# A hybrid attention and RWKV-7 layer: how the planner emits side work, where pair set-up waits, and where the gates stand

## The chip, the cores and the metric

The kernel runs on one core of one Trainium2 chip. The metric is the device time of one execution in microseconds; each kernel is run several times and the median is taken. One further execution is profiled, and its trace gives the rows below. In the rows PE is TensorE (PEld its weight loads), DVE is VectorE, ACT is ScalarE, POOL is GpSimd, and SPq is the DMA queue that SyncE (SP) issues to. TensorE's clock has two levels, 1.2 and 2.4 GHz; the rows show the granted level as 0.50 or 1.00.

## The reference

One decoder layer over 512 tokens of width 2048, in float32. An RMS norm of `x`, then one input projection (2048 x 8480) whose columns are attention q, k, v and gate z, the RWKV-7 columns r, k, v with three low-rank parts, and the RWKV gate z. Attention has 16 heads of 64 with rotary q and k, and mixes three dilated causal windows. RWKV-7 has 16 heads whose 64 x 64 state follows

```
sa    = state @ a_t
state = state * w_t + outer(sa, b_t) + outer(v_t, k_t)
y_t   = state @ r_t
```

with the decay `w_t` between 0 and 1 from data, `a_t = -kk`, `b_t = kk * a`, `kk` normalised per head. The result is normalised per head, a bonus is added, and it is multiplied by its low-rank gate `g`. Each branch is multiplied by `silu(z)`; both are concatenated and go through one output projection (2048 x 2048), the residual is added, and a final RMS norm follows.

## The kernel before

All large products are done in pairs of rounded parts: the activations are held as `hth` + `htl`, each weight chunk is loaded as `raw` and split into `whi` (ScalarE) and `wlo` (VectorE), and three matmuls (`hh,whi`, `hl,whi`, `hh,wlo`) make one product. A projection of 128 columns ("main matmuls" `mm_r`, `mm_k`, `mm_v`, `mm_z`, `mm_qk`) is 16 x 3 = 48 matmuls of 128x512. Chunks are loaded and split ahead by `Feeder.tick` at fixed places of this stream (AHEAD = 2 chunks).

The stream of main matmuls is written out by hand in `items` (lines 1215 to 1275): the low-rank columns and k0, then for pair p = 0 to 7 (two RWKV heads of 64 on 128 partitions) k, r and v, with some z projections of the attention gate between; the rest of z0 to z6; `gl128`; three blocks of v for attention (`mv`); 16 blocks of q and k; z8 to z15 (RWKV gates); z7; and then the output projection `mo`, `mh`, `mt` over 16 mixed tiles.

Everything else is a Python generator in `sides`, and `pump` (line 353) runs these between main matmuls while the program is written. `Model` keeps a planned clock: TensorE's calls move it, each other engine has a planned `busy` time from a fixed cost and a cost per element, and a generator's `yield (delay, tile or engine)` sets when it is due again on that clock. Nothing of this runs on the chip: it fixes the order in which each engine's queue is filled. Engines take their queues in order and wait for each other by semaphores. `until(cond)` moves the planned clock in steps of 0.2 us and runs only sides until the condition holds; `drain()` runs sides until none is left; `after(2, f)` runs `f` two matmuls later.

For each pair the sides are:

- `pre(p)`: the normaliser, decays `W` = exp(-cum) and `wi` = exp(cum), the tiles `bt` and `Fa`, the matmuls `pM`, from which `mc` goes to DRAM (`md`) and comes back as the table `Mp`; then the bonus `bn`, and after pair p-1 is `built` the tiles `L`, `X`, `FT` and `A`.
- `subst(p)`, called the solve here: on POOL 31 steps of two products each (`Xtmp`, `XT`) invert the triangles held in `Mp`. Each step needs the one before. It ends in `solved`, and XT goes through DRAM (`xq`).
- `merges(p)`, `build(p)`, `scan(p)`: small matmuls (`zpb`, `zf`, `gp`) that end in `built`, then eight scan steps `Y` one after another, each with two copies on ScalarE or VectorE, which end in `scanned`; then the head's norm, and the tile goes to DRAM as y.

Buffers come from rings: `k2` (20 tiles of 128x512), `k1` (6 small ones), `k4` (9). `shift_evac` takes a projection out of PSUM: a memset of one column of `u` on POOL, a product with `rstd` into `u`, and two operations that make `d`. The z0 to z6 gates go to DRAM (`spill_out`) and come back in `att` (`fetch_y`); z7's is applied after attention. `gate_g(p)` loads the low-rank gate's weights `gw`, splits them (`gh`, `gl`), multiplies (`pg`) and scales the reloaded y; `gate(8+p)` then applies z. `pre_mix` drains, reloads seven attention tiles and starts `mix_split`, which splits the 16 mixed tiles for the output projection in the order `KO` (RWKV first).

Of the kernel before, what the change touches and what calls it, by code (L numbers as in the profile page):

```python
# [11 lines left out]
F32 = mybir.dt.float32  # L12
# [3 lines left out]
ALU = mybir.AluOpType  # L16
# [25 lines left out]
class Model:  # L42


    def __init__(self):
        self.clock, self.ready, self.read = 0.0, {}, {}

# [15 lines left out]
class Engine:  # L63
    def __init__(self, model, eng, fixed, rate):
        self.model, self.eng, self.fixed, self.rate, self.busy = model, eng, fixed, rate, 0.0

    def cost(self, op, o, args):
        rate = self.rate
        if op == "reciprocal":
            rate = 0.0062  # L70
        elif op == "memset":
            return 0.04 + 0.0009 * math.prod(o.shape[1:])
        elif op in ("tensor_scalar", "tensor_copy") and self.fixed == 0.07:
            rate = 0.0006
        return self.fixed + rate * math.prod((args[0] if op == "tensor_reduce" else o).shape[1:])

# [16 lines left out]
class Tensor(Engine):  # L93
# [4 lines left out]
    def __getattr__(self, op):  # L98
        fn = getattr(self.eng, op)

        def call(o, lhs, rhs, **kw):
            m = self.model
            rows = o.shape[0]
            load = rows * 0.00084
            passes = 2 if rhs.dtype != F32R and op == "matmul" else 1
            hold = math.prod(rhs.shape[1:]) * (1 if rhs.dtype == F32R else 2) / 2400
            if rows < P and o.offset >= 64 * 512:
                hold, passes = 0.02, 1
            w = max(m.after([], [lhs, rhs]), m.read.get(o.name, 0.0))
            for _ in range(passes):  # L110
                self.start = max(m.clock, self.start + load, w)
                m.clock = self.start + hold + 0.003
            m.done(m.clock, [o], [lhs, rhs], 0.2)
            return fn(o, lhs, rhs, **kw)  # L114
        return call
# [14 lines left out]
def hymba_kernel(ctx: ExitStack, tc: tile.TileContext, xT, x, wa, wb, wo, pv, w2a2, g2, fg,  # L130
# [3 lines left out]
    model = Model()  # L134
    V = Engine(model, nc.vector, 0.07, 0.00104)
    S = Engine(model, nc.scalar, 0.06, 0.00095)
    G = Engine(model, nc.gpsimd, 0.15, 0.0020)
    TE = Tensor(model, nc.tensor)
# [11 lines left out]

    K1N, K2N, K4N, RAWN, AHEAD = 6, 20, 9, 2, 2

# [41 lines left out]
    def prologue():  # L194
# [7 lines left out]
        def squares():  # L202
            for k in range(KT):
# [5 lines left out]
                if k % 2:  # L209
                    yield 0.0, S  # L210
            yield 0.0, acc
            yield from rms(acc)
# [140 lines left out]
    def pump():  # L353
# [4 lines left out]
        for s_ in sorted(sides, key=lambda s: (s[2], s[1])):  # L358
            while s_[1] <= model.clock and credit[0] > (-DEBT, 0, -99.0)[s_[2]]:
                t = model.clock  # L360
                try:
                    wait = next(s_[0])
# [165 lines left out]
    def shift_evac(src, mu, name, rows=P, scaled=True):  # L528
        u = k2([P, T + 1], f"u_{name}")
        G.memset(u[:rows, 0:1], 0.0)  # L530
        if scaled:
# [77 lines left out]
    def pre(p, r, k, v):  # L609
# [71 lines left out]
        Q.dma_start(md.rearrange("c p t -> p c t"), mc)  # L681
        while p >= 1 and p - 1 not in solved:
            yield 0.5
# [12 lines left out]
        V.scalar_tensor_tensor(rk, r, col("r_k", p), k, ALU.mult, ALU.mult)  # L696
        yield 0.1, rk
        rh, rl = hilo(rk, f"rk{p}")
        yield 0.1, rl
# [11 lines left out]
        for h in range(2):  # L711
            S.copy(X[h][H[h], :, H[h]], ident[H[h], H[h]][:, None, :].to_broadcast([64, NCH, C]))
            V.tensor_tensor(L[h][H[h], :, H[1 - h]], c3(k)[H[h]], wi[H[h]], ALU.mult)
            G.tensor_tensor(X[h][H[h], :, H[1 - h]], c3(r)[H[h]], W[H[h], :, 1:C + 1], ALU.mult)
        yield 0.1, L[0], L[1]
# [26 lines left out]
    def subst(p, Mp, rn2):  # L742
        while p >= 1 and p - 1 not in solved:
            yield 0.287
        V.tensor_tensor(Mp, Mp, rn2[:, None, :].to_broadcast([P, 32, 32]), ALU.mult)
        XT = sp.tile([P, 8, 32], F32, tag="XT", bufs=1, name=f"XT{p}")
        tmp = sp.tile([P, 8, 32], F32, tag="Xtmp", bufs=1, name=f"Xtmp{p}")
        G.memset(XT, 0.0)
        for g in range(4):
            V.tensor_copy(XT.rearrange("p c t -> p (c t)")[32 * g:32 * g + 32, 8 * g:8 * g + 232:33],  # L750
                          rn2[32 * g:32 * g + 32, 8 * g:8 * g + 8])
        yield 0.1, XT
        for j in range(31):
            n = 31 - j
# [366 lines left out]

    KO = list(range(8, 16)) + list(range(8))
    mh, ml = [], []
# [91 lines left out]
    add_aa((0, 9), ("lora", "k0"), (lora_evac, lambda a: rkv_evac(0, "k", 8, a)))  # L1215
    NZ, EARLY = 7, {2: 1, 3: 1, 4: 1, 5: 1, 6: 1}
    zs = iter(range(NZ))
# [7 lines left out]
    for p in range(NP):  # L1225
        add_z(EARLY.get(p, 0))
        add_call(lambda p=p: until(lambda: p < 3 or p - 3 in scanned))
        if p:
# [17 lines left out]
    for p in range(NP):  # L1246
        add_call(lambda p=p: start(gate_g(p), 0.21))
        add_a(50 + p, f"z{8 + p}", lambda a, p=p: gate(8 + p, a))
    for p in range(NZ, NP):
        add_call(lambda p=p: fetch_y(p, f"o{p}"))  # L1250
        if p == NP - 1:
            add_call(lambda: pre_mix())
        add_a(42 + p, f"z{p}", lambda a, p=p: gate(p, a))

    def pre_mix():
# [57 lines left out]
def _layout(inp):  # L1313
# [27 lines left out]
    wo = f["w_out"][0].reshape(KT, P, 4, 512)  # L1341
    wo = wo[list(range(8, 16)) + list(range(8))].transpose(2, 1, 0, 3)
    mu = f["shift_mu"][0]
# [41 lines left out]
```

## Time and profile before

| | |
|---|---|
| median of 3 runs | 1188.93 us (1188.77 to 1189.62) |
| the profiled execution | 1189.53 us, its span 1187.7 us |
| mean granted TensorE clock | 0.982 |
| TensorE busy | 1144.1 us (96%) |
| VectorE busy | 738.8 us (62%) |
| ScalarE busy | 537.2 us (45%) |
| POOL busy | 354.2 us (30%) |

The span runs from the first to the last instruction of the profiled execution, and the rest of its own time lies around it. Busy time of TensorE is the union of its matmuls, whose ends overlap, so a busy TensorE need not be one at its peak. A line number such as L114 or L86 is that of the planner's wrapper through which every matmul or vector operation passes, so rows are told apart by the names of their tiles.

### The profile page before, as it was taken

What the parts mean: (1) busy time and instruction counts of PE and PEld (TensorE: products, weight loads), DVE (VectorE), ACT (ScalarE), POOL (GpSimd) and SP (SyncE); (2) the same over time, 40 slices, a digit from 0 to 9 for tenths busy, and PEclk for the clock granted to TensorE, in tenths of its full rate; (3) what the DMA queues carried; (4) which work ended last, traced back from release to release, by engine and by line L of the source; (5) the groups of instructions that cost most, each with busy time, mean ns of one, the idle gap of its engine ahead of it and who ended that gap; (6) DMA issues with size and microseconds to landing.
All of it is one profiled execution on the core that took longest, in us unless ns stands there. A gap on an engine that the chain in (4) does not pass through costs nothing. (4 is left out here: it accounts for less than half of the span.)

```text
span 1187.7 us, 19122 instructions
## 1 busy us (share of the span) xinstructions
PE 1144.1 (96%) x6878; PEld 948.2 (80%) x6878; DVE 738.8 (62%) x1475; ACT 537.2 (45%) x1196; POOL 354.2 (30%) x629
## 2 busy tenths in 40 slices
PE   7899999999999989979999999999999999999997
PEld 5687877787787778858899888888887878888897
DVE  6678667777886756786745455666667646334252
ACT  6354536555535545554534323445345434223133
POOL 1007566574838082383800021110010000011010
PEclk9899999999999979998999999999999999999999
DMA  7243333424241414314233544444354336344333
GB/s 259 82 117 113 97 108 87 123 71 125 74 137 55 139 46 116 108 59 111 58 96 90 163 125 146 132 127 127 116 154 133 113 107 217 113 140 121 110 125 142
DMA packets 89583, 139.10 MB, mean 117 GB/s; under 512 B 37904, under 2 KB 47632, under 8 KB 89488
## 3 DMA queue, kind: packets, MB, share of 16 engines
q1 hardware_dynamic: 89056, 137.31, 38.3%
q8 instruction: 54, 0.88, 0.3%
q10 hardware_dynamic: 432, 0.58, 0.1%
q14 instruction: 41, 0.34, 0.1%
HBM read 114.18 MB, written 14.48 MB: 108 GB/s over the span
## 5 line engine op out<-in xcount | busy, mean ns | idle before, releaser
L86 POOL TENSOR_TENSOR Xtmp<-XT,Mp 128x248 f32<-128x248 f32 (+30 forms) x248 | 127.9, 516 | 126.9 <-DVE XT L86 109.0
L86 POOL TENSOR_TENSOR XT<-XT,Xtmp 128x248 f32<-128x248 f32 (+30 forms) x248 | 139.8, 564 | 21.1 <-DVE XT L86 2.1
L114 PE MATMUL mm_z<-hl,whi 128*128 128x512 f32 x256 | 103.3, 404 | 0.0
L114 PE MATMUL mm_z<-hh,whi 128*128 128x512 f32 x256 | 102.9, 402 | 0.0
L114 PE MATMUL mm_z<-hh,wlo 128*128 128x512 f32 x256 | 102.4, 400 | 0.0
L114 PE MATMUL mm_qk<-hh,whi 128*128 128x512 f32 x256 | 100.6, 393 | 0.8 <-ACT gtok L86 0.8
L114 PE MATMUL mm_qk<-hh,wlo 128*128 128x512 f32 x256 | 100.8, 394 | 0.0
L114 PE MATMUL mm_qk<-hl,whi 128*128 128x512 f32 x256 | 100.4, 392 | 0.0
L86 DVE TENSOR_TENSOR wlo<-raw_o,whi 128x512 fp32r<-128x512 f32 x64 | 48.1, 793 | 83.4 <-ACT whi L86 83.3
L86 POOL TENSOR_TENSOR y<-y,fg 128x512 f32<-128x512 f32 (+1 forms) x16 | 19.3, 1242 | 264.4 <-ACT mo L86 245.7
L86 ACT ACTIVATE ss<-ss,nm 128x128 f32<-128x128 f32 (+3 forms) x64 | 35.5, 555 | 101.4 <-DVE nm L86 101.4
L86 ACT ACTIVATE whi<-raw_o 128x512 fp32r<-128x512 f32 x64 | 36.8, 623 | 92.6 <-PE mo L114 69.9
L86 POOL TENSOR_TENSOR m<-m,m 128x512 f32<-128x512 f32 x16 | 23.0, 1457 | 185.6 <-DVE m L86 161.4
L114 PE MATMUL mv<-whi,hh 128*128 128x352 f32 x192 | 64.8, 337 | 10.9 <-DVE u_gl L86 9.5
L114 PE MATMUL mo<-whi,mh 128*128 128x512 f32 x192 | 74.7, 389 | 0.0
L114 PE MATMUL mo<-wlo,mh 128*128 128x512 f32 x192 | 74.7, 389 | 0.0
L114 PE MATMUL mo<-whi,ml 128*128 128x512 f32 x192 | 74.7, 389 | 0.0
L86 DVE TENSOR_TENSOR wlo<-raw_qk,whi 128x512 fp32r<-128x512 f32 x64 | 48.5, 783 | 36.5 <-ACT whi L86 34.3
L86 DVE TENSOR_TENSOR wlo<-raw_v,whi 128x352 fp32r<-128x352 f32 (+1 forms) x80 | 49.2, 630 | 34.7 <-ACT whi L86 34.0
L114 PE MATMUL mv<-wlo,hh 128*128 128x352 f32 x192 | 64.0, 333 | 0.0
L86 DVE TENSOR_TENSOR wlo<-raw_z,whi 128x512 fp32r<-128x512 f32 x64 | 47.4, 766 | 26.3 <-ACT whi L86 26.0
L114 PE MATMUL mv<-whi,hl 128*128 128x352 f32 x192 | 63.4, 330 | 0.0
(297 smaller groups left out, 3024.2 us busy)
## 6 DMA issues: line engine op xcount, KB each, us to landing
raw_z<-in_wa_dram SPq DMA_DIRECT2D x32, 512.0 KB
raw_qk<-in_wa_dram SPq DMA_DIRECT2D x32, 512.0 KB
raw_o<-in_wo_dram SPq DMA_DIRECT2D x32, 512.0 KB
raw_v<-in_wb_dram SPq DMA_DIRECT2D x24, 352.0 KB
raw_r<-in_wa_dram SPq DMA_DIRECT2D x16, 512.0 KB
raw_v<-in_wa_dram SPq DMA_DIRECT2D x16, 512.0 KB
raw_k<-in_wa_dram SPq DMA_DIRECT2D x15, 512.0 KB
xk<-in_xT_dram SPq DMA_DIRECT2D x16, 256.0 KB
```

The lines of the kernel that those rows point to most:

```text
L86: return fn(o, *args, **kw)
L114: return fn(o, lhs, rhs, **kw)
```

## The change

The planner's costs are new: each TensorE matmul of the rounded type moves the planned clock by 0.0135 us beyond its columns instead of 0.003, a change of matmul shape by 0.1, VectorE and ScalarE have a least cost (0.18, 0.25), and POOL's cost is 0.30 + 0.0028 per element instead of 0.15 + 0.0020. `pump` starts no step of a side with rank 0 or 1 while VectorE or ScalarE is planned busy for more than 3 us ahead. `Mp` is loaded once pair p-2 is solved instead of p-1, and `subst` scales it and sets up XT (now two buffers) before it waits for solve p-1. In `pre`, r and k are multiplied by `W` and `wi` in place on all 128 partitions, and their halves are copied into `X` and `L`. The memset in `shift_evac` is on VectorE. `k1` has five buffers. All eight attention gates z0 to z7 are projected in the recurrent part, one ahead of each of pairs 2 to 7, and pairs 4 to 7 wait for pair p-3 to be built where pairs 3 to 7 waited for it to be scanned. `pre_mix` stands before z15, and the output projection takes its mixed tiles in the order 0 to 15. The rms step of the start is due 2 us of plan later.

```diff
--- before.py
+++ after.py
@@ -43,7 +43,7 @@
     def __init__(self):
-        self.clock, self.ready, self.read = 0.0, {}, {}
+        self.clock, self.mode, self.ready, self.read = 0.0, None, {}, {}
@@ -61,8 +61,9 @@
 class Engine:
-    def __init__(self, model, eng, fixed, rate):
+    def __init__(self, model, eng, fixed, rate, least=0.0):
         self.model, self.eng, self.fixed, self.rate, self.busy = model, eng, fixed, rate, 0.0
+        self.least = least
@@ -72,7 +73,8 @@
             rate = 0.0006
-        return self.fixed + rate * math.prod((args[0] if op == "tensor_reduce" else o).shape[1:])
+        n = math.prod((args[0] if op == "tensor_reduce" else o).shape[1:])
+        return max(self.least, self.fixed + rate * n)
@@ -107,9 +109,14 @@
             w = max(m.after([], [lhs, rhs]), m.read.get(o.name, 0.0))
+            mode = (lhs.shape[0], rows)
+            if mode != m.mode:
+                m.clock += 0.1
+                m.mode = mode
+            gap = 0.0135 if rhs.dtype == F32R else 0.003
             for _ in range(passes):
                 self.start = max(m.clock, self.start + load, w)
-                m.clock = self.start + hold + 0.003
+                m.clock = self.start + hold + gap
             m.done(m.clock, [o], [lhs, rhs], 0.2)
@@ -132,9 +139,9 @@
     model = Model()
-    V = Engine(model, nc.vector, 0.07, 0.00104)
-    S = Engine(model, nc.scalar, 0.06, 0.00095)
-    G = Engine(model, nc.gpsimd, 0.15, 0.0020)
+    V = Engine(model, nc.vector, 0.07, 0.00106, 0.18)
+    S = Engine(model, nc.scalar, 0.06, 0.00095, 0.25)
+    G = Engine(model, nc.gpsimd, 0.30, 0.0028)
     TE = Tensor(model, nc.tensor)
@@ -148,7 +155,7 @@
-    K1N, K2N, K4N, RAWN, AHEAD = 6, 20, 9, 2, 2
+    K1N, K2N, K4N, RAWN, AHEAD = 5, 20, 9, 2, 2
@@ -208,7 +215,7 @@
                     yield 0.0, S
-            yield 0.0, acc
+            yield 2.0, acc
             yield from rms(acc)
@@ -358,6 +365,8 @@
                 t = model.clock
+                if s_[2] >= 0 and max(V.busy, S.busy) > t + 3.0:
+                    break
                 try:
@@ -527,7 +536,7 @@
         u = k2([P, T + 1], f"u_{name}")
-        G.memset(u[:rows, 0:1], 0.0)
+        V.memset(u[:rows, 0:1], 0.0)
         if scaled:
@@ -679,7 +688,7 @@
         Q.dma_start(md.rearrange("c p t -> p c t"), mc)
-        while p >= 1 and p - 1 not in solved:
+        while p >= 2 and p - 2 not in solved:
             yield 0.5
@@ -695,6 +704,8 @@
         yield 0.1, rk
+        V.tensor_tensor(c3(r), c3(r), W[:, :, 1:C + 1], ALU.mult)
+        V.tensor_tensor(c3(k), c3(k), wi, ALU.mult)
         rh, rl = hilo(rk, f"rk{p}")
@@ -710,8 +721,8 @@
             S.copy(X[h][H[h], :, H[h]], ident[H[h], H[h]][:, None, :].to_broadcast([64, NCH, C]))
-            V.tensor_tensor(L[h][H[h], :, H[1 - h]], c3(k)[H[h]], wi[H[h]], ALU.mult)
-            G.tensor_tensor(X[h][H[h], :, H[1 - h]], c3(r)[H[h]], W[H[h], :, 1:C + 1], ALU.mult)
+            evac(L[h][H[h], :, H[1 - h]], c3(k)[H[h]])
+            evac(X[h][H[h], :, H[1 - h]], c3(r)[H[h]])
         yield 0.1, L[0], L[1]
@@ -740,16 +751,16 @@
     def subst(p, Mp, rn2):
-        while p >= 1 and p - 1 not in solved:
-            yield 0.287
         V.tensor_tensor(Mp, Mp, rn2[:, None, :].to_broadcast([P, 32, 32]), ALU.mult)
-        XT = sp.tile([P, 8, 32], F32, tag="XT", bufs=1, name=f"XT{p}")
+        XT = sp.tile([P, 8, 32], F32, tag="XT", bufs=2, name=f"XT{p}")
         tmp = sp.tile([P, 8, 32], F32, tag="Xtmp", bufs=1, name=f"Xtmp{p}")
...
         yield 0.1, XT
+        while p >= 1 and p - 1 not in solved:
+            yield 0.1
         for j in range(31):
@@ -1119,7 +1130,7 @@
-    KO = list(range(8, 16)) + list(range(8))
+    KO = list(range(16))
     mh, ml = [], []
@@ -1213,7 +1224,7 @@
     add_aa((0, 9), ("lora", "k0"), (lora_evac, lambda a: rkv_evac(0, "k", 8, a)))
-    NZ, EARLY = 7, {2: 1, 3: 1, 4: 1, 5: 1, 6: 1}
+    NZ, EARLY = 8, {2: 1, 3: 1, 4: 1, 5: 1, 6: 1, 7: 1}
     zs = iter(range(NZ))
@@ -1224,7 +1235,7 @@
         add_z(EARLY.get(p, 0))
-        add_call(lambda p=p: until(lambda: p < 3 or p - 3 in scanned))
+        add_call(lambda p=p: until(lambda: p < 4 or p - 3 in built))
         if p:
@@ -1245,13 +1256,9 @@
         add_call(lambda p=p: start(gate_g(p), 0.21))
-        add_a(50 + p, f"z{8 + p}", lambda a, p=p: gate(8 + p, a))
-    for p in range(NZ, NP):
-        add_call(lambda p=p: fetch_y(p, f"o{p}"))
         if p == NP - 1:
             add_call(lambda: pre_mix())
-        add_a(42 + p, f"z{p}", lambda a, p=p: gate(p, a))
-
+        add_a(50 + p, f"z{8 + p}", lambda a, p=p: gate(8 + p, a))
     def pre_mix():
@@ -1339,7 +1346,7 @@
     wo = f["w_out"][0].reshape(KT, P, 4, 512)
-    wo = wo[list(range(8, 16)) + list(range(8))].transpose(2, 1, 0, 3)
+    wo = wo.transpose(2, 1, 0, 3)
     mu = f["shift_mu"][0]
```

## Rows read from the trace of the kernel before

**Rows 1.** The page, part 1: busy us, share of the span, instructions.

```profile
PE 1144.1 (96%) x6878; PEld 948.2 (80%) x6878; DVE 738.8 (62%) x1475; ACT 537.2 (45%) x1196; POOL 354.2 (30%) x629
```

**Rows 2.** Busy time by stretch: length, busy us (instructions) by engine, PEclk, DMA.

```profile
core 0: us, PE busy (x) PEld busy (x) DVE busy (x) ACT busy (x) POOL busy (x), PEclk, DMA share, GB/s
43.20:50.00 6.80, 6.80 (x19) 5.54 (x20) 4.09 (x20) 0.00 (x0) 0.00 (x0) 0.50 0.51 151
...
155.80:159.20 3.40, 3.40 (x10) 2.63 (x9) 2.45 (x8) 0.88 (x2) 2.59 (x4) 0.50 0.20 17
...
330.00:360.00 30.00, 30.00 (x230) 24.13 (x228) 24.57 (x50) 13.26 (x27) 14.75 (x22) 1.00 0.42 115
...
413.65:422.10 8.45, 6.83 (x59) 5.80 (x57) 6.89 (x16) 6.02 (x13) 6.85 (x10) 1.00 0.44 141
422.10:435.62 13.52, 10.83 (x56) 8.93 (x57) 4.55 (x8) 3.97 (x11) 12.38 (x20) 0.50 0.13 39
435.62:439.10 3.48, 3.48 (x37) 2.71 (x37) 2.21 (x4) 1.09 (x2) 3.01 (x7) 0.50 0.00 0
...
531.30:541.50 10.20, 5.12 (x17) 5.13 (x18) 7.51 (x21) 4.88 (x11) 2.32 (x12) 0.50 0.30 72
690.00:960.00 270.00, 269.71 (x1334) 219.20 (x1333) 171.45 (x427) 125.30 (x347) 19.99 (x14) 1.00 0.43 128
```

**Rows 3.** Timeline of TensorE: start, duration, operation, idle time before it and releaser.

```profile
42.69 1.45 PE L114 MATMUL pr<-ones,acc 128*128 128x1 f32 x8 [3.59 <-DVE acc L86]
...
154.15 0.69 PE L114 MATMUL zpb<-xd,zsb 32*32 32x32 f32 x32 [1.93 <-DVE zsb L86]
...
324.16 1.15 PE L114 MATMUL pM<-Fa,bt 64*64 64x64 f32 x32 [1.90 <-DVE wc L86]
...
415.23 4.05 PE L114 MATMUL gp<-X,L 128*128 128x128 f32 x32
...
435.62 0.77 PE L114 MATMUL mm_k<-hh,whi 128*128 128x512 f32 x1
...
536.38 0.66 PE L114 MATMUL mv<-whi,hh 128*128 128x352 f32 x1 [9.45 <-DVE u_gl L86]
```

**Rows 4.** Waits of TensorE: total us, times, longest us.

```profile
PE pF L114 <- DVE L L86: 2.9, 6, 1.1
```

**Rows 5.** Timeline of VectorE around 535 us.

```profile
535.63 0.69 DVE L86 TENSOR_TENSOR u_gl<-mm_gl,rstd 128x512 f32<-128x512 f32 x1
```

**Rows 6.** Timelines of POOL and SP's queue, from solve 4 to solve 5.

```profile
386.82 0.24 POOL L86 TENSOR_TENSOR XT<-XT,Xtmp 128x8 f32<-128x8 f32 x1
...
408.50 1.73 SPq L126 DMA_DIRECT2D Mp<-md  x4
...
414.27 0.61 POOL L86 TENSOR_TENSOR Xtmp<-XT,Mp 128x248 f32<-128x248 f32 x1 [22.68 <-DVE XT L86]
...
454.75 0.22 POOL L86 TENSOR_TENSOR XT<-XT,Xtmp 128x8 f32<-128x8 f32 x1
```

**Rows 7.** Instruction groups, 60 to 660 us: count | busy us, mean ns | idle before.

```profile
L86 POOL TENSOR_TENSOR Xtmp<-XT,Mp 128x248 f32<-128x248 f32 (+30 forms) x248 | 127.9, 516 | 126.9 <-DVE XT L86 109.0
L86 POOL TENSOR_TENSOR X<-d_r,W 64x512 f32<-64x512 f32 x16 | 21.3, 1331 | 0.6
L86 DVE TENSOR_TENSOR L<-d_k,wi 64x512 f32<-64x512 f32 x16 | 17.3, 1080 | 0.3
L86 ACT COPY X<-csts 64x512 f32<-64x512 f32 x16 | 9.8, 613 | 0.1
```

**Rows 8.** Timelines of SP's queue, TensorE and VectorE around z15.

```profile
976.39 2.49 SPq L126 DMA_DIRECT2D gw<-in_g_dram  x5
...
980.45 0.39 PE L114 MATMUL mm_z<-hh,whi 128*128 128x512 f32 x1
...
982.77 0.69 DVE L86 SCALAR_TENSOR_TENSOR yl<-zt,yl 128x512 f32<-128x512 f32 x1
...
987.19 0.60 DVE L86 TENSOR_TENSOR gl<-gw,gh 128x128 fp32r<-128x128 f32 x2
...
991.33 0.39 PE L114 MATMUL pg<-g128h,gh 128*128 128x512 f32 x1
```

## The prediction

> **What bounds the kernel now.** The page's busy table comes first: TensorE is busy 1144.1 of 1187.7 us [rows 1]. At most 43.6 us of idle time is left, and any gain must come from there or from stretches in which the same matmuls run at a lower clock. So the table of windows is read next, for busy time and granted clock by stage [rows 2]. From 690 to 960 us TensorE is busy 269.71 of 270 us at clock 1.00: nothing can be won there, only lost. The losses sit before 660 us, in the recurrent part, and the timeline of TensorE names them one by one [rows 3]. I price each as idle time plus half of what was busy at clock 0.50 (1.2 instead of 2.4 GHz).
>
> - Start, 39 to 50 us: 3.59 idle, waiting for `acc` on VectorE, then 6.80 busy at 0.50, costing 3.40. Together 7.0.
> - 152 to 159: 1.93 idle for `zsb`, then 3.40 at 0.50, costing 1.70. Together 3.6.
> - 324: 1.90 idle for `wc`, without a fall of the clock in the rows that follow.
> - 413.65 to 439.10: no main matmul starts before 435.62, only small ones such as `gp`. Busy are 6.83 at full clock, 10.83 and 3.48 at half, which is 6.83 + 5.42 + 1.74 = 14.0 of work in 25.45. Loss 11.5.
> - 526 to 541: 9.45 idle for `u_gl`, then 5.12 busy at 0.50, costing 2.56. Together 12.0.
> - Short waits of the `pF` matmuls for `L`: 2.9 in six places [rows 4].
>
> The sum is 38.9 us. That is all the change can win in the stages it touches, unless it also removes work, and it removes no matmul.
>
> **Why the two large losses are there.** At 413 the list stands in an `until` (line 1227): pair 7's projections wait until pair 4 is scanned. Only the scan's chain of small matmuls is left to issue, each waiting for a copy on ScalarE or VectorE, and the clock falls. At 526 the last `mv` group needs the PSUM bank that `u_gl` empties. VectorE reaches `u_gl` only at 535.63 [rows 5]. Line 1235 had held the main matmuls until pair 7 was `half` done, which line 682 ties to the end of solve 6, and meanwhile everything that was ready had been put on VectorE ahead of `u_gl`.
>
> Behind both is the solve on POOL. Its last step of pair 4 ends at 387.06 and the first of pair 5 starts at 414.27, of which POOL spent 22.68 waiting for VectorE's `XT`; the table load `Mp` was issued only at 408.50 [rows 6]. Over six such places these waits are 109.0 us [rows 7]. Pair 5's 62 steps take until 454.75 + 0.22 = 454.97, which is 40.7 us or 0.656 a step. For the mean step of 128 elements the planner before books 0.15 + 0.0020 x 128 = 0.406 us, so it takes a solve for done some 15 us early; the one after books 0.30 + 0.0028 x 128 = 0.658, which is the pitch.
>
> **The change part by part.**
>
> *Set-up during the solve, second `XT`.* The load of `Mp`, its scaling and the diagonal move ahead of the wait for solve p-1. The gap of 27.2 us goes to the hand-over alone, so a solve follows the last after about 1 us. A solve then needs 40.7 us of each pair's time, but inputs come slower: a pair has 4 x 48 main matmuls at 0.2267 (z15: 48 from 980.45 to 991.33, [rows 8]), 43.5 us, and some 14 to 17 us of small ones (14.0 stood in the stretch from 413.65): about 60 us, an estimate. So TensorE paces the solves. By itself this part is worth nothing; it makes the conditions of the list true early. The four `Mp` loads and the `md` store of each pair go earlier on SP ahead of weight loads: the row shows 1.73 us for four, inside the two chunks (10.9 us of matmuls) by which weights are loaded ahead. Free.
>
> *`until` loosened to `p < 4 or p - 3 in built`, one gate moved forward.* `built` is true when the `gp` matmuls end, at 415.23 + 4.05 = 419.3 for pair 4, 16 us before 435.62, and one more z projection (10.9 us) stands before it. With solves earlier by tens of us the condition holds on arrival. Of the 11.5 I take 10.5, since scan steps still wait now and then.
>
> *Backlog limit of 3 us, costs nearer the trace.* At 526 the queue ahead of `u_gl` shrinks from about 9 us to 3 at most; `half` no longer waits for solve 6. I leave 1.5 us of idle time without a fall of the clock: 10.5 of 12.0. The bounds of what stays are 0 and 4 (3 of backlog and `u_gl` itself). The waits at 152 and 324 are of the same kind, VectorE late against the plan: half of each, 1.8 + 1.0. At the start the rms step is put off by 2.0 us of plan, but each matmul now moves the plan by 0.0105 more, 1.26 over the 120 or so issued by then (two projections and half a third). It moves some 3 matmuls, 0.75 us; I take 1.0 of the 7.0 (bounds 0 and 7).
>
> *Decays multiplied in place.* Two `L` products (1080 ns each) and two POOL `X` products (1331) go; two full-width products (0.69 to 1.08, by `u_gl` and `L`) and four copies come (613 ns, by ScalarE's copy into `X`) [rows 5, 7]. VectorE and ScalarE together gain 1.4 to 2.2 + 2.5 - 2.2, so 1.7 to 2.5 us a pair, POOL loses 2.7. It hides under TensorE's 61 us, since VectorE is busy 24.57 of 30 there, 50 of 61 [rows 2]; uncovered it would be 8 x 2.5 = 20. `pF` waits for copies instead of products: I take 2 of the 2.9. The 25 one-column memsets that come to VectorE are not in the rows there; between 0 and 0.3 us (under half of `u_gl`), 7.5 us at most in 400, are off the path, and they take away POOL's queue as a thing `d_*` waits for.
>
> *Order of the output's weights, `mix_split` from 0.* The last mixed tile is again the one gated last, needed after 15/16 of the first output sweep. No cost.
>
> *`pre_mix` moved ahead of z15.* This is the one thing that gets worse. `pre_mix` drains, and `gate_g(7)` has just been started, so its `pg` matmuls must issue with no z matmul to cover them. Before, pair 7's gate had z15 over it. Z14 ends where z15 begins, at 980.45; the `gw` loads were issued from 976.39, z14's own gate holds VectorE until 982.77 + 0.69 = 983.46, and `gl` takes 0.60: `pg` cannot start before 984.1 [rows 8]. Idle 3.7 us. The nearest idle stretches (3.59 and 1.93) were followed by 6.80 and 3.40 us at 0.50, costing 3.4 and 1.7; I take 2.4 between them. Cost 6.1; bounds 2 (if all of it runs ahead of TensorE) and 10 (if the loads start only at 980.45: 2.49 us of issue and their landing on top). Queued behind on SP are eight reloads `yl` and output weights; they have all of z15.
>
> The sum: 10.5 + 10.5 + 1.8 + 1.0 + 1.0 + 2.0 - 6.1 = 20.7. The profiled execution took 1189.53 us (span 1187.7 and 1.8 around it), 0.6 over the median of 1188.93. 1189.5 - 20.7 = 1168.8, by the median 1168.
>
> **Rivals.**
>
> *All waits vanish and the last gate is covered*: 38.9 less, so 1150 to 1158. For it: costs that match the pitch. Against: the start is hardly touched. Chance 0.15.
>
> *The waits come back elsewhere*: half of the two large items and the small ones return as waits of scan steps and of `u_gl`, and the drain costs 8: 1189.5 - 13.4 + 8 = 1184, up from 1176. Chance 0.12.
>
> *VectorE held behind POOL* (slower): the `XT` diagonal needs POOL's memset of `XT`, which now stands in POOL's queue amid the running solve; VectorE, in order, waits, and weight splits behind it. Two chunks, 10.9 us, cover it. With 0.658 against 0.656 the hold is one or two steps, 1.5 to 3 us. Seven times 16 us held would cost 7 x 5 = 35 and give 1204; it decides from about 14 us. Chance 0.06.
>
> *VectorE becomes the bound* (slower): `L`, 512 columns, takes 1080 ns where POOL's product runs beside it, `u_gl` of as many columns 690. From 330 to 360 us VectorE is busy 24.57 with POOL busy for half of the time, 14.75 [rows 2]. With POOL busy all of it, and if all of VectorE's work were such products, it would grow by 1.57 / 1.28 to 30.1 of 30: just at the bound. Copies and transposes are no such products, so it stays below. Each per cent beyond would cost 0.6 us a pair, 5 us in all; past 4% the gain is gone, 1195 at 5%. Chance 0.04. The Trainium skill, GPSIMD Engine Reference, section Key points, says that POOL shares its SBUF interfaces with VectorE and contends with its two-input instructions, which speaks against solves without a pause; the 1080 against 690 ns agrees.
>
> *Nothing changes*: the chain on POOL was never TensorE's limit and the waits stay. 1189. The 22 us without a main matmul speak against it. Chance 0.03.
>
> **Numbers.** The forecast has 0.60 and its own range of 1160 to 1176. With the larger gain (0.15) and most of the smaller (0.12) the range is 1151 to 1182. Faster by over 0.2% (2.4 us, about what a measurement of this kernel tells from no change) 0.87, within 0.03, slower 0.10.
>
> **What would show it.** Right: POOL's wait for `XT` between solves falls from 109 us to under 20; main matmuls run through where pair 7's projections start; the idle time ahead of the fourth `mv` tile is under 2 us; a new idle stretch of 3 to 4 us with a half clock behind it stands before the `pg` of pair 7, in front of the last z. Wrong: TensorE waits for `whi` or `wlo` in the recurrent part, VectorE waits for `XT` of POOL for over 5 us, or 690 to 960 us is no longer full.

## The result, and the profile after

The changed kernel takes 1173.14 us (median of 4 runs, 1169.45 to 1174.68) against 1188.85 us of the kernel before beside it (4 runs): ratio 0.9866, 95% interval 0.9840 to 0.9892. The forecast was 1168 with a range of 1151 to 1182. The profiled execution took 1172.79 us, with a span of 1170.7 us and a mean granted clock of 0.990. The profile is read in the order used for the kernel before, first part 1 of the page.

```profile
PE 1133.5 (97%) x6878; PEld 943.2 (81%) x6878; DVE 760.2 (65%) x1521; ACT 544.0 (46%) x1209; POOL 333.9 (29%) x586
```

Against [rows 1] TensorE has as many matmuls and is busy 10.6 us less. The spans differ by 17.0 us, so 6.4 us came from idle time. Of the 10.6, the clock explains 5.5: by the windows, 29.6 us were busy at 0.50 before and 18.6 are now, at half their length; the other 5.1 weren't traced to a stretch, since matmuls overlap and their ends are modelled. The windows of the kernel after show where (columns as in [rows 2]).

```profile
44.78:48.19 3.41, 3.41 (x10) 2.63 (x9) 3.17 (x14) 0.00 (x0) 0.00 (x0) 0.50 0.74 198
351.98:355.39 3.41, 3.41 (x9) 2.26 (x7) 3.29 (x6) 2.74 (x5) 3.02 (x6) 0.50 0.50 177
418.87:423.66 4.79, 2.51 (x35) 1.91 (x33) 4.76 (x7) 2.65 (x7) 3.16 (x7) 1.00 0.33 62
423.66:430.49 6.83, 4.90 (x23) 4.90 (x24) 3.69 (x8) 4.34 (x9) 2.63 (x4) 0.50 0.27 96
478.27:481.69 3.42, 3.42 (x39) 2.37 (x37) 2.78 (x8) 2.31 (x6) 2.97 (x8) 0.50 0.60 215
526.00:541.00 15.00, 14.85 (x113) 13.62 (x112) 12.40 (x31) 6.68 (x16) 2.69 (x4) 1.00 0.43 127
660.00:960.00 300.00, 300.00 (x1477) 243.04 (x1476) 186.97 (x454) 132.88 (x363) 22.55 (x16) 1.00 0.43 129
973.20:976.62 3.42, 3.42 (x9) 2.67 (x9) 2.58 (x4) 0.80 (x2) 0.00 (x0) 0.50 0.95 347
```

The stretch at 526, which cost 12.0 us before, is full at clock 1.00. The stretch ahead of pair 7's projections is half as long as before, but it is there. Three short stretches at 0.50 are new, and the timeline of TensorE has an idle time ahead of each (columns as in [rows 3]).

```profile
42.61 1.05 PE L121 MATMUL pr<-ones,acc 128*128 128x1 f32 x8 [2.69 <-DVE acc L88]
...
350.54 0.69 PE L121 MATMUL zpb<-xd,zsb 32*32 32x32 f32 x32 [1.79 <-DVE zsb L88]
...
425.59 6.16 PE L121 MATMUL gp<-X,L 128*128 128x128 f32 x32 [4.21 <-DVE L L88]
431.51 0.49 PE L121 MATMUL mm_k<-hh,whi 128*128 128x512 f32 x1
...
477.34 0.69 PE L121 MATMUL zpb<-xnb,mo 32*32 32x32 f32 x32 [1.75 <-DVE xnb L88]
...
971.39 0.50 PE L121 MATMUL pg<-g128h,gh 128*128 128x512 f32 x1 [1.75 <-ACT gh L88]
...
972.74 0.50 PE L121 MATMUL pg<-g128h,gl 128*128 128x512 f32 x1 [0.62 <-DVE gl L88]
```

With the prediction's own price, idle time plus half of what is busy at 0.50, its terms come out so (the wait for `wc` stands at 84 us now; a stop is a stretch in which no main matmul starts):

| term of the prediction | predicted | measured | from |
|---|---|---|---|
| stop ahead of pair 7 | 10.5 | 4.8 | 12.64 us (418.87 to 431.51) hold 2.51 + 4.90/2 + 1.02 = 6.0 of work: 6.7 lost, before 11.5 |
| `u_gl` | 10.5 | 12.0 | no wait, clock 1.00 |
| the waits at 152 and 324 | 2.8 | -3.3 | 5.5 before; now 1.79 + 1.7, 1.75 + 1.7 and 1.8 for `wc` = 8.8 |
| start | 1.0 | 2.6 | 2.69 + 1.7 = 4.4, before 7.0 |
| `pF` | 2.0 | 2.0 | 2.9 to 0.9 |
| `pre_mix` drains before z15 | -6.1 | -4.1 | 1.75 + 0.62 + 1.7 |
| sum | 20.7 | 14.0 | the spans differ by 17.0 |

The terms hold 8.5 us of idle time and 5.5 of half clock. As idle time fell by 6.4 us only, it grew by 2.1 outside the terms, although the waits of `Y` for `A` fell from 5.4 to 1.4 us. The remaining 3.0 us are thus the untraced 5.1 less these 2.1.

The prediction named one sign first: POOL's wait for `XT` was to fall from 109 us to under 20. The groups of the kernel after, from 60 to 660 us, show 165.2 (columns as in [rows 7]; the products with `W` and `wi` and the copies of their halves are in the same view).

```profile
L88 POOL TENSOR_TENSOR Xtmp<-XT,Mp 128x248 f32<-128x248 f32 (+30 forms) x248 | 128.9, 520 | 182.6 <-DVE XT L88 165.2
...
L88 DVE TENSOR_TENSOR d_k<-d_k,wi 128x512 f32<-128x512 f32 x8 | 5.9, 741 | 0.0
L88 DVE TENSOR_TENSOR d_r<-d_r,W 128x512 f32<-128x512 f32 x8 | 5.5, 690 | 0.0
L88 DVE COPY L<-d_k 64x512 f32<-64x512 f32 x8 | 5.7, 716 | 0.1
L88 ACT COPY L<-d_k 64x512 f32<-64x512 f32 x8 | 4.9, 614 | 0.0
```

Neither total is one of hand-overs alone. Each holds the wait ahead of the first solve, which follows no other, and the 109.0 lacks the last two hand-overs of the kernel before, where a product `yb` stood in POOL's queue ahead of the first step. First POOL's timeline before, then after:

```profile
94.39 0.62 POOL L86 TENSOR_TENSOR Xtmp<-XT,Mp 128x248 f32<-128x248 f32 x1 [26.88 <-DVE XT L86]
...
553.62 1.28 POOL L86 TENSOR_TENSOR yb<-yb,bnl 128x512 f32<-128x512 f32 x1 [16.70 <-ACT yb L86]
```

```profile
100.06 0.62 POOL L88 TENSOR_TENSOR Xtmp<-XT,Mp 128x248 f32<-128x248 f32 x1 [44.74 <-DVE XT L88]
...
537.80 0.62 POOL L88 TENSOR_TENSOR Xtmp<-XT,Mp 128x248 f32<-128x248 f32 x1 [19.52 <-DVE XT L88]
```

From the last step of one solve to the first of the next, the seven hand-overs of these timelines take 164.0 us before and 128.5 after. They became shorter by a fifth, and are far from under 20. One of them shows why: the timelines of POOL, TensorE, SP's queue and VectorE from the end of solve 4 to the start of solve 5, after.

```profile
373.87 0.22 POOL L88 TENSOR_TENSOR XT<-XT,Xtmp 128x8 f32<-128x8 f32 x1
...
393.05 1.15 PE L121 MATMUL pM<-Fa,bt 64*64 64x64 f32 x32
...
400.22 1.74 SPq L133 DMA_DIRECT2D Mp<-md  x4
...
407.19 1.22 DVE L88 TENSOR_TENSOR Mp<-Mp,rn 128x1024 f32<-128x1024 f32 x1
...
408.56 0.62 POOL L88 TENSOR_TENSOR Xtmp<-XT,Mp 128x248 f32<-128x248 f32 x1 [34.23 <-DVE XT L88]
```

Nothing of pair 5 waits here for solve 4. Its `pM` comes 19 us after solve 4 has ended, and from there the table goes to DRAM and back and is scaled, another 15. The first solve starts at 100.06 and the last at 537.80, one in 62.5 us, and the first seven take 44.2 in the mean (the eight from 37 to 55); that leaves 18.4 us a pair, seven times.

### The profile page after: what moved, and what is told of

It reads as the page before. It is cut to its first block, busy times and chain, and to the rows that moved or that the text cites. A ratio compares the mean times of both kernels' runs of the same rounds, so it can differ in the third digit from the quotient of the medians.

```text
span 1170.7 us, 19091 instructions
## 1 busy us (share of the span) xinstructions
PE 1133.5 (97%) x6878; PEld 943.2 (81%) x6878; DVE 760.2 (65%) x1521; ACT 544.0 (46%) x1209; POOL 333.9 (29%) x586
## 5 line engine op out<-in xcount | busy, mean ns | idle before, releaser
L88 POOL TENSOR_TENSOR Xtmp<-XT,Mp 128x248 f32<-128x248 f32 (+30 forms) x248 | 128.9, 520 | 182.6 <-DVE XT L88 165.2
L88 POOL TENSOR_TENSOR XT<-XT,Xtmp 128x248 f32<-128x248 f32 (+30 forms) x248 | 142.2, 573 | 21.4 <-DVE XT L88 2.5
L88 DVE TENSOR_TENSOR wlo<-raw_v,whi 128x352 fp32r<-128x352 f32 (+1 forms) x80 | 50.0, 655 | 26.9 <-ACT whi L88 26.4
L88 DVE TENSOR_TENSOR wlo<-raw_z,whi 128x512 fp32r<-128x512 f32 x64 | 47.9, 766 | 18.8 <-ACT whi L88 18.4
```

What stands on the lines that cost most here:

```text
L88: return fn(o, *args, **kw)
```

## The experiments

Two theories stood against each other. One was the prediction's: the loosened `until` takes away the stop, the limit of 3 us takes away the wait for `u_gl`, the set-up alone is worth nothing. The other gave the gain to the costs and the set-up, with the limit as a loss. All kernels compute the whole reference. Ratios are to the kernel before, with 95% intervals.

**The limit out.**

```diff
-                if s_[2] >= 0 and max(V.busy, S.busy) > t + 3.0:
-                    break
```

> The changed kernel without the limit of 3 us on planned backlog. Theory A (the limit holds back the steps of pre, so that pM and Mp come late and POOL starves, and in return it keeps VectorE's queue short): POOL's wait for XT falls from 165.2 us to under 90, the main matmuls' stop at pair 7 (12.6 us from 418.87) shortens by more than half, but waits for products on VectorE come back; time 1168 to 1180. Theory B (inputs are late because VectorE itself is full, the limit only writes down what happens anyway): POOL's wait stays within 20 us of 165, time within 2 us of 1173.

1168.88 us, 0.9830 (0.9809 to 0.9850), about 4 us faster than with it, with intervals that still touch. The window of its stop, then POOL's wait (total, times, longest) and one row of POOL's timeline:

```profile
413.58:423.08 9.50, 7.20 (x99) 6.38 (x99) 7.11 (x13) 5.34 (x11) 5.15 (x9) 1.00 0.48 140
```

```profile
POOL Xtmp L88 <- DVE XT L88: 127.2, 6, 42.9
...
206.16 0.62 POOL L88 TENSOR_TENSOR Xtmp<-XT,Mp 128x248 f32<-128x248 f32 x1 [24.25 <-DMA xd<-xq]
```

TensorE has no wait for `u_gl` here either, so the limit isn't what removed it. The stop is 9.5 us long instead of 12.6, not less than half, but it loses 2.3 us where the changed kernel lost 6.7: all of it idle, 1.79 of it ahead of `zpb`, at full clock, and `gp` has no wait for `L`. What it wins there it gives back in part at the start, where 6.8 us at 0.50 follow the wait for `acc` instead of 3.4. POOL's 127.2 us leave out one wait of the same step, which the profile puts down to a DMA; with its 24.25 they are 151.5. The limit accounts for 14 of POOL's 165 us, and the fall to under 90 did not come.

**The set-up back behind the solve.**

```diff
-        while p >= 2 and p - 2 not in solved:
+        while p >= 1 and p - 1 not in solved:
             yield 0.5
...
     def subst(p, Mp, rn2):
+        while p >= 1 and p - 1 not in solved:
+            yield 0.287
...
-        while p >= 1 and p - 1 not in solved:
-            yield 0.1
```

> The changed kernel with the set-up of the next solve put back behind the end of the solve before it (load of Mp, scaling, diagonal). Theory A (the set-up by itself is worth nothing, since POOL waits for inputs anyway; only where half is tied to a solve does it matter): solves after a pause are unmoved, solve 1 starts some 15 us later, time 1173 to 1177. Rival (the chain of solves sets when pairs are built, and thus the stop of the main matmuls): the stop at pair 7 grows from 12.6 to over 20 us and time goes to 1182 or more.

1175.82 us, 0.9892 (0.9865 to 0.9919): not told apart from the changed kernel by the time, but the timeline has the wait again, followed by 6.8 us at 0.50.

```profile
533.60 0.66 PE L121 MATMUL mv<-whi,hh 128*128 128x352 f32 x1 [6.32 <-DVE u_gl L88]
```

The second solve starts 15 us later, as expected, but those after it are not unmoved: they start 8 to 24 us later, and the seven hand-overs take 169.8 us where the changed kernel has 128.5. Pair 7's stop, with the limit in place, loses nothing; three new stops of 11 to 13 us, from 222, 289 and 358 us, lose 3 to 4 us each. The window of pair 7's:

```profile
425.25:430.85 5.60, 5.60 (x65) 5.43 (x65) 5.04 (x9) 1.16 (x2) 5.06 (x8) 1.00 0.60 185
```

**The last gate under z15 again, `pre_mix` before it as in the change.**

```diff
-        add_call(lambda p=p: start(gate_g(p), 0.21))
         if p == NP - 1:
             add_call(lambda: pre_mix())
+        add_call(lambda p=p: start(gate_g(p), 0.21))
```

> The changed kernel with pre_mix called just before the last low-rank gate is started instead of just after, so that its drain does not hold that gate's matmuls. Theory A (the drain's wait, 1.8 + 0.6 idle and 3.4 us of half clock at 969 to 977, is pure loss of some 4.4 us): 1168 to 1170, no idle time of TensorE above 1 us after 660 us. Rival (the wait moves to the first output matmuls, since reloads and splits start no earlier): 1172 to 1174.

1167.43 us, 0.9816 (0.9800 to 0.9833), 5.7 us below the changed kernel. The window over everything from the queries and keys into the output projection is full:

```profile
660.00:1140.00 480.00, 479.88 (x2376) 396.40 (x2376) 261.21 (x566) 190.56 (x482) 42.43 (x32) 1.00 0.44 133
```

The drain's price is real: 4.1 us in the trace, 5.7 by the times, 6.1 predicted.

**The changed kernel with all of the planner's old costs.**

```diff
-                m.clock += 0.1
...
-            gap = 0.0135 if rhs.dtype == F32R else 0.003
+            gap = 0.003
...
-    V = Engine(model, nc.vector, 0.07, 0.00106, 0.18)
-    S = Engine(model, nc.scalar, 0.06, 0.00095, 0.25)
-    G = Engine(model, nc.gpsimd, 0.30, 0.0028)
+    V = Engine(model, nc.vector, 0.07, 0.00104)
+    S = Engine(model, nc.scalar, 0.06, 0.00095)
+    G = Engine(model, nc.gpsimd, 0.15, 0.0020)
```

> The changed kernel with the planner's costs of before (limit and all else kept). Theory A (costs nearer the trace are what keeps TensorE from being sent to matmuls whose operands are late): waits of TensorE on VectorE in the recurrent part grow by 8 us or more, time 1180 to 1190. Rival (the limit and the loosened conditions carry the gain, the costs little): 1171 to 1176.

1191.97 us (10 runs), 1.0023 (1.0010 to 1.0037): the whole gain is gone. The window from 516 to 600 us, with 11.5 us idle and a clock of 0.84, is enough for that loss; the same stretch of the changed kernel stands below it:

```profile
516.00:600.00 84.00, 72.51 (x576) 66.27 (x575) 52.46 (x106) 33.12 (x79) 35.90 (x76) 0.84 0.27 70
...
516.00:600.00 84.00, 82.89 (x645) 76.87 (x643) 57.95 (x126) 43.08 (x99) 34.06 (x67) 1.00 0.35 95
```

**The kernel before with the new costs and nothing else** (the lines above the other way).

> The kernel before with the planner's new costs alone (TensorE's gap and change of shape, least costs, POOL's cost). Theory A (the costs carry most of the gain: old costs in the changed kernel lost all of it): 1172 to 1180, the waits for zsb and wc gone or halved. Rival (true costs pay only together with the loosened conditions; with the old ones a later planned end of each solve makes the conditions hold later): 1187 or more, and the stretches without a main matmul grow from the 22 us at pair 7.

1233.35 us, 1.0383 (1.0364 to 1.0401), 46 us slower than the kernel before beside it. The window shows the first of the five stretches that now hold no main matmul, and below it stands the longest wait.

```profile
166.03:194.00 27.97, 23.21 (x227) 20.02 (x227) 16.04 (x29) 10.44 (x24) 24.27 (x40) 0.69 0.14 40
```

```profile
PE mv L121 <- DVE u_gl L88: 14.9, 1, 14.9
```

The five stretches are 120.6 us long in all, with 97.5 busy at clocks of 0.69 to 0.77, and the old `until` holds five pairs, 3 to 7. By the code, a planner that books more time for POOL finds pair p-3 scanned later, and issues only the scan's chain until then.

**The kernel before with the limit alone.**

```diff
                 t = model.clock
+                if s_[2] >= 0 and max(V.busy, S.busy) > t + 3.0:
+                    break
```

> The kernel before with the limit of 3 us on planned backlog alone. Theory A (the limit starves pre and frees nothing that half and solve 6 do not hold anyway): 1189 to 1200, POOL's wait for XT above 109 us, the wait for u_gl at most halved. Rival (the limit is what shortens VectorE's queue ahead of u_gl, as the prediction had it): 1176 to 1181, the wait for u_gl under 3 us.

1192.82 us, 1.0040 (1.0023 to 1.0056): slower. The wait for `u_gl` is halved, and pair 7's stop is shorter, 13.8 us without a main matmul instead of 21.8. Waits elsewhere take back more: `pF` waits for `L` 5.1 us (2.9 before [rows 4]) and `zpb` for `xnb` 3.4 (0.4 before).

```profile
PE pF L114 <- DVE L L86: 5.1, 7, 1.8
PE mv L114 <- DVE u_gl L86: 4.7, 1, 4.7
...
PE zpb L114 <- DVE xnb L86: 3.4, 1, 3.4
```

**The kernel before with the loosened `until` and one gate ahead of pair 7.**

```diff
-    NZ, EARLY = 7, {2: 1, 3: 1, 4: 1, 5: 1, 6: 1}
+    NZ, EARLY = 7, {2: 1, 3: 1, 4: 1, 5: 1, 6: 1, 7: 1}
...
-        add_call(lambda p=p: until(lambda: p < 3 or p - 3 in scanned))
+        add_call(lambda p=p: until(lambda: p < 4 or p - 3 in built))
```

> The kernel before with the loosened condition (p < 4 or pair p-3 built) and one more z projection ahead of pair 7, nothing else. Theory A (the stop at pair 7 is worth the 11.5 us that the prediction priced): 1177 to 1180, main matmuls run through at 413. Rival (the stop only moves to the next condition, half of pair 7, since solves are not sooner): 1185 to 1190, and the wait for u_gl or a stretch without main matmuls before mv grows.

1178.86 us, 0.9925 (0.9909 to 0.9942). Its windows and the timeline show that the stop answers to these two lines, and the other large loss in part: 405 to 445 is full, and the wait for `u_gl` is 1.67 us where it was 9.45 [rows 3]. But from 513 to 531 us still 5.7 us are idle, ahead of `pM`, `zpb` and `mv`, and 5.4 are busy at 0.50: 8.5 lost of the 12.0.

```profile
405.00:445.00 40.00, 39.49 (x269) 31.40 (x270) 29.89 (x50) 22.32 (x48) 32.53 (x55) 1.00 0.25 76
...
513.00:531.00 18.00, 12.26 (x107) 10.79 (x106) 13.50 (x37) 9.28 (x22) 3.02 (x14) 0.81 0.42 98
```

```profile
525.20 0.66 PE L114 MATMUL mv<-whi,hh 128*128 128x352 f32 x1 [1.67 <-DVE u_gl L86]
```

**The same with the set-up**: `Mp` after solve p-2, two `XT`, the wait for p-1 behind the scaling, `k1` of five.

```diff
-    K1N, K2N, K4N, RAWN, AHEAD = 6, 20, 9, 2, 2
+    K1N, K2N, K4N, RAWN, AHEAD = 5, 20, 9, 2, 2
...
-        while p >= 1 and p - 1 not in solved:
+        while p >= 2 and p - 2 not in solved:
             yield 0.5
...
     def subst(p, Mp, rn2):
-        while p >= 1 and p - 1 not in solved:
-            yield 0.287
...
         yield 0.1, XT
+        while p >= 1 and p - 1 not in solved:
+            yield 0.1
```

> The kernel before with the loosened condition, the z projection ahead of pair 7 and the set-up of the next solve ahead of the end of the running one, with old costs and without the limit. Theory A (set-up adds what tying half to solve 6 cost, and with the condition makes most of the gain without new costs): 1170 to 1175. Rival (with old costs earlier inputs only pile more on VectorE, as the old costs did in the changed kernel): 1180 to 1192.

1179.88 us, 0.9928 (0.9910 to 0.9945), against 0.9925 without: by itself the set-up is worth nothing. That is near the rival's 1180 and far from the 1170 to 1175 hoped for. POOL waits 154.2 us (139.9 without), the wait for `u_gl` stays 1.7.

**The changed kernel with POOL's old cost alone.**

```diff
-    G = Engine(model, nc.gpsimd, 0.30, 0.0028)
+    G = Engine(model, nc.gpsimd, 0.15, 0.0020)
```

> The changed kernel with the old cost of POOL alone (0.15 + 0.0020 per element); TensorE's, VectorE's and ScalarE's costs stay new. Theory A (of the costs it is the solve's planned length that matters: with it too short, merges are sent to TensorE before XT is there): 1183 to 1192, waits of TensorE before zpb, zf and gp grow by 8 us or more. Rival (it is TensorE's own planned time that matters, which without the gap and the change of shape lags the real one and lets sides fall behind): 1170 to 1177.

1186.25 us (10 runs), 0.9987 (0.9974 to 0.9999). Of the 1.6% that all old costs lose, this one line loses 1.2%. Its waits:

```profile
PE gp L121 <- ACT L L88: 7.0, 4, 2.5
...
PE zpb L121 <- DVE zsb L88: 4.4, 1, 4.4
```

The changed kernel has no wait of `gp` for ScalarE, and 1.8 us of `zpb` for `zsb`. What TensorE waits for is the work that follows a solve (`zpb`, then `gp`). By the code, with too short a cost for POOL the planner takes a solve for done before it is, and places that work too early in TensorE's queue; the waits fit that, but make up only part of the 13 us lost.

**Without the limit, and the last gate under z15**: the edits of the first and the third experiment in one kernel.

```diff
-                if s_[2] >= 0 and max(V.busy, S.busy) > t + 3.0:
-                    break
...
-        add_call(lambda p=p: start(gate_g(p), 0.21))
         if p == NP - 1:
             add_call(lambda: pre_mix())
+        add_call(lambda p=p: start(gate_g(p), 0.21))
```

> The changed kernel without the limit and with pre_mix ahead of the last low-rank gate's start; the rms step as in the change. Theory A (the two gains lie in different stages and add, and it was the later rms step that spoilt their sum by shifting all that follows in the plan): 1163 to 1165. Rival (without the limit the reordered end brings nothing, or the other way round): 1167 to 1170.

1162.36 us (5 runs, 1159.2 to 1167.8), 0.9778 (0.9754 to 0.9802): the fastest kernel of the study, 10.8 us below the changed one where the two edits alone gave 4.3 and 5.7. The second half is as full as in the third experiment. Its stop loses 4.2 us although the limit is out: 2.4 idle, and 3.4 busy at 0.50.

```profile
413.93:425.19 11.26, 8.82 (x99) 7.84 (x99) 7.25 (x13) 5.75 (x12) 6.54 (x12) 0.85 0.51 144
```

**That, with the rms step of the start due 5 instead of 2 us of plan later.**

```diff
-            yield 2.0, acc
+            yield 5.0, acc
```

> The changed kernel without the limit, with pre_mix ahead of the last low-rank gate's start, and the rms step due 5 instead of 2 us of plan later. If the three add (4.3 and 5.7 measured, and 2.7 idle plus 1.7 or more of half clock at the start): 1159 to 1163. If the start's wait only moves, since all later evacuations wait for the norm: 1163 to 1165.

1169.99 us, 0.9854 (0.9837 to 0.9872), slower than the 0.9778 without the edit and outside both expectations. The windows show that the start is mended: no idle time, clock 1.00. But what follows has shifted: the stop ahead of pair 7 loses 6.8 us, and `zpb` waits 8.8 us in five places, where it waited 6.1 in four.

```profile
36.00:60.00 24.00, 24.00 (x109) 19.61 (x108) 18.17 (x47) 8.38 (x16) 0.35 (x2) 1.00 0.30 94
415.35:429.03 13.68, 9.66 (x98) 8.38 (x99) 9.94 (x16) 7.35 (x15) 7.61 (x12) 0.75 0.38 119
```

**The fastest kernel with two gates ahead of pair 7.**

```diff
-    NZ, EARLY = 8, {2: 1, 3: 1, 4: 1, 5: 1, 6: 1, 7: 1}
+    NZ, EARLY = 8, {2: 1, 3: 1, 4: 1, 5: 1, 6: 1, 7: 2}
```

> As the kernel without the limit and with the last low-rank gate covered, and with two z projections instead of one ahead of pair 7. Theory A (what is left of the stop at pair 7, 9.3 us without a main matmul of which some 5.4 are zf and gp that have to run anyway, plus half of 3.4 us at half clock, is a lack of main matmuls ahead of the condition, and 10.9 us more of them fill it): some 4 to 5.6 us less, 1157 to 1159, and no stretch of over 2 us without a main matmul there. Rival (work that is put ahead of pair 7 is missed later, when its solve is the last and only mv covers it, and the waits return there): 1161 to 1165.

1170.81 us, 0.9846 (0.9823 to 0.9869), outside both expectations. The stop is gone, 415 to 435 holds 19.37 of 20 us at 1.00, and 100 us later a worse one stands, as the window and the timeline show (without the edit this window holds 19.84 of 20 us at 1.00):

```profile
513.00:533.00 20.00, 13.12 (x74) 11.84 (x73) 14.08 (x39) 11.76 (x27) 0.00 (x0) 0.66 0.37 90
```

```profile
519.36 1.93 PE L121 MATMUL pM<-Fa,bt 64*64 64x64 f32 x31 [4.12 <-DVE rt_gn L88]
```

By the list, a z projection used at 415 is one less for later; that this lack is the cause at 519 is argued, not tried.

## Why the prediction was right, and where its sum was off

**What bounds the kernel: right.** The gain lies before 660 us, and 11.9 of its 17.0 us are idle time and half-clock time of TensorE, where the account of 38.9 us looked for it. The other 5.1 are in no term. The forecast came within some 5 us with luck: its terms gave 14.0 instead of 20.7, the stop and the waits falling short by 11.8, `u_gl`, the start and the drain giving 5.1 back, and 3.0 came from where nothing had been priced.

**The mis-sized term: "Of the 11.5 I take 10.5", the stop ahead of pair 7.** It returned 4.8. The step behind it, "with solves earlier by tens of us the condition holds on arrival", failed twice. The condition hangs on pair 4, and its solve ended 13 us earlier, at 374.09 instead of 387.06, not tens. And pair 4 was built later for all that: its `gp` ended at 431.75, before at 419.28. The end of the solve did not set it. `zpb` of pair 4 came 20 us after, `zf` only in the stop itself, and `gp` then waited 4.21 us for `L`, whose copies stood behind other pairs' work on VectorE:

```profile
421.27 0.70 DVE L88 STREAM_TRANSPOSE yt<-yc 128x512 f32<-128x512 f32 x1
...
424.84 1.30 DVE L88 COPY L<-zf 64x512 f32<-64x512 f32 x2
```

In the kernel before, the loosened condition and one gate, with nothing else changed, take the stop away. In the changed kernel it came back, and no single edit owns it. Without the limit it loses 2.3 us, but 4.2 and 6.8 in the two other kernels without the limit that have one gate ahead of pair 7; with the limit and without the set-up it loses nothing.

**"Under 20" for POOL's wait contradicted the prediction's own pace.** The part on the set-up put a pair at about 60 us and a solve at 40.7, so each solve must leave POOL some 19 us idle, seven times 135 in all; the closing list then asked for under 20. Measured are 62.5 us a pair and 128.5 in the seven hand-overs: the pace was right and the sign wrong. The 109.0 that it started from was misread too, as 26.9 of it come before the first solve. The step "by itself this part is worth nothing" stood on the pace and held: 0.9928 against 0.9925. In the changed kernel the set-up does more: without it the hand-overs are 41 us longer and the wait for `u_gl` is back at 6.3 us, though the time hardly differs.

**The gain at `u_gl` was right in size and half right in its cause.** The prediction gave it to the limit's shorter queue and to `half`, which no longer waits for solve 6. The first isn't needed: without the limit the wait stays away. The second is, by the second experiment. In the kernel before, the limit alone leaves 4.7 us of 9.5 and the loosened condition alone 1.7, each with 6.8 us at 0.50 around it. No single edit owns these 12 us.

**The limit was taken for a gain and is a loss**: 0.4% slower alone in the kernel before; without it the changed kernel runs some 4 us faster, and the one with the last gate under z15 some 5.

**The costs had no term of their own, and should have had.** The prediction used them only to say that the planner's 0.658 us for a step matches 0.656 on the chip. Old costs in the changed kernel lose 19 us, the new ones alone in the kernel before lose 46. This fits a pair: with a truer cost of POOL the planner knows when a condition is false, so the condition must be one that TensorE can afford to wait for. The kernel before with both the new costs and the loosened condition, and nothing else, wasn't run.

**The waits at 152 and 324, predicted +2.8, were -3.3.** Those two went, and others of their kind came at 350 and 477, both with a half clock behind them. The rival in which the waits come back was right here alone; 1184 us was too much, since `u_gl` did not come back.

**The drain: right in place, 4.1 us instead of 6.1.** The prediction held the first `pg` until `gl` was there. The first `pg` matmuls need `gh` alone, from ScalarE, and started at 971.39; `gl` then held the next for 0.62. The 3.42 us at half clock cost 1.7, the lower of the two prices that the prediction took its 2.4 from.

**In-place products: no cost seen, as predicted.** The products took 741 and 690 ns, the copies 610 to 716 in the mean (`X` from `d_r`, 633 on VectorE), and the one-column memsets on VectorE 0.06 us, near the lower of the two bounds. VectorE and ScalarE are busy 28 us more than before, above the 14 to 20 of the sum and the 1.5 of the memsets; TensorE never lacked a weight part in the recurrent stage for more than 0.3 us, so neither of the slower rivals came. POOL's product of half as many partitions took 1331 ns [rows 7]. The Trainium skill, GPSIMD Engine Reference, section Key points, puts VectorE at about twice POOL's speed for elementwise work; 1331 against 690 agrees. Against VectorE's product of the same shape in the same stage, 1080 [rows 7], the factor is 1.2.

**Open.** Why `pM` of some pairs comes only after the solve before has ended is not settled: the limit carries 14 of POOL's 165 us. Nor is why the stop ahead of pair 7 goes in some of these kernels and stays in others. Which of the other new costs makes the quarter of their gain that isn't POOL's wasn't separated. The memset, the order of the mixed tiles and the in-place products weren't tried by themselves.

## What to carry to other kernels

When an order is planned in advance, make its costs true and its conditions loose together: here truer costs alone lost three times what the whole change won, and looser conditions alone won about half of it. Removing one wait moves the order of all that comes after it, so read the whole stage again after each edit, and keep a piece of independent work for the place where the next wait will stand. Check the signs that you name against your own rates: a stage fed every 60 us that needs 41 must wait.

## What the runs showed of the hardware

Idle times of almost the same length had different ends. In the kernel before, 1.93 us at 154 was followed by 3.40 us at 0.50 and 1.90 us at 324 by none; after, 1.75 us at 477 and 1.79 at 350 were each followed by 3.4, and the 1.8 us for `wc` at 84 by none. Without the limit 1.79 us at 414, as long as the wait at 350, was followed by none. In the kernel before with the loosened `until`, 1.67 us for `u_gl`, behind two others of 2.35 and 1.71 within 8 us, came with 6.8 us at 0.50. A wait of this length can't be priced by its idle time; its half clock may be as much again or more.

The copies of 64 x 512 elements in float32 took VectorE 633 to 716 ns in the mean and ScalarE 610 to 614, but VectorE's means hide 419 to 1471 ns. In the changed kernel POOL was at work during every one of them; the longest stood beside one of its products. In the kernel without the limit, POOL was idle from 181.9 to 206.16 us, and three copies there took 412 to 424 ns, two thirds of ScalarE's time. Two of them from VectorE's timeline without the limit, then VectorE and POOL in the changed kernel:

```profile
186.57 0.41 DVE L88 COPY X<-d_r 64x512 f32<-64x512 f32 x1
187.00 0.42 DVE L88 COPY L<-d_k 64x512 f32<-64x512 f32 x1
```

```profile
234.80 1.47 DVE L88 COPY L<-d_k 64x512 f32<-64x512 f32 x1
...
234.69 1.30 POOL L88 TENSOR_TENSOR yb<-yb,bnl 128x512 f32<-128x512 f32 x1 [9.22 <-ACT yb L88]
```
